# A state space model computed by parts of four tokens instead of token by token

## The chip, the cores and the metric

The kernel runs on one core of a Trainium2 chip. The metric is the device time of one execution in microseconds (us); of several runs the median counts. The core has TensorE (PE, matrix products), VectorE (DVE), ScalarE (ACT), GpSimd (POOL) and SyncE (SP, which issues most DMAs). Each engine works through its own list of instructions strictly in order.

## What is computed

256 tokens of width 1024 go through two blocks of two layers each. The change concerns the second block. Each of its layers is a feed-forward, a token mixer and another feed-forward, with norms and a modulation between. The token mixer contains a state space model on 512 of its channels, in 32 groups of 16 channels with 64 complex states each:

```python
def token_mixer(h, w_in, ...):
    u, q, k, v, f, g_a, g_b = jnp.split(h @ w_in, cuts, axis=-1)
    y_ssm = s5_ssm(u, a_re, a_im, log_dt, b_re, b_im, c_re, c_im, d_skip)
    z_val, z_gate = jnp.split(jax.nn.gelu(y_ssm) @ glu_w, 2, axis=-1)
    y_a = z_val * jax.nn.sigmoid(z_gate)
    y_b = forgetting_attention(q, k, v, f + forget_b) @ attn_w_out
    return (jax.nn.sigmoid(g_a) * y_a + jax.nn.sigmoid(g_b) * y_b) @ w_out

def s5_ssm(u, ...):
    lam_bar = jnp.exp(lam * dt)                     # per group and state, complex
    bu = einsum('blgn,gpn->blgp', u, b_bar)         # 16 inputs -> 64 states, each token
    # states[t] = lam_bar * states[t-1] + bu[t], t over the 256 tokens
    y = real(einsum('gnp,blgp->blgn', c, states))   # 64 states -> 16 outputs
    return y + d_skip * u
```

## The kernel before

**Weights.** Everything stays on the core but the weights, which stream from memory as 576 blocks of 128 rows by 1024. `prepare` (L210) issues a block's DMA on SP into `wr` (L223), ScalarE casts it to the high part `wh` (L229), and VectorE computes the low part `wl = wr - wh` (L236). The pools hold four `wr`, five `wh` and four `wl`. `group` (L255 to L266) makes 24 products of 256 columns from a block, three for each pair of tiles (`xh·wh`, `xl·wh`, `xh·wl`), into tiles `g` of PSUM. The modulation (L496) is computed on VectorE beside this, a step of 128x1024 at a time, from `mraw`.

**Feed-forward.** Groups of gate and up products alternate; behind an up group, VectorE multiplies its results into `act` (L440), ScalarE casts them to `ah` (L367), VectorE computes `al` (L368), and the down products follow.

**Token mixer** (`mixer2`, L1241). First the projection of `u`, then `settle` (L131 to L138), which finishes the normalised activations: for each of eight tiles a step into a buffer `xs` of a ring of two, ScalarE's rounding to `xh`, and a step to `xl`. L1279 scales `u` by the norm `rho` (L404), L1280 adds a bias, and `split` makes a high and a low part of it. A narrow product (`narrow`, L306 and L311) in four column groups gives the forget gates. The projections of v, q, k and two gates follow, with the state space model and the attention between them.

**State space model.** `ssm_params` (L1075) prepares each layer's coefficients: a table of rotations (cosine `c` and sine `z`) for 128 tokens, and the scaled matrix `cT`. Layer 0's is emitted in the block's first feed-forward, layer 1's at the start of its layer, with five DMAs of 512 KB on POOL. `ssm_pair` (L1128) works 16 times a layer, on two groups of 64 states: four DMAs for each two pairs gather `u` into `ux` (L1145); two products (L1147) give the inputs of 128 states at 256 tokens, real and imaginary; VectorE turns them with the table (L1133), runs the recurrence as scans of 128 tokens (L1158) in two halves with a small turning step between (L1166, L1168), and turns the states back (L1133); two float32 products in a group of 32 columns (L1179, L1180) give the outputs. When four pairs are through, `ydone` (L1293) takes over.

**Order.** A planner in the kernel (class `Order`, L1549) gives every instruction a price, schedules the program as a list with these prices, several times forward and backward, and fixes the shortest plan's order on each engine. Tiles of one ring are handed out in the order in which the code was written.

Of the kernel before, what the change touches and what calls it, by code (L numbers as in the profile page):

```python
# [8 lines left out]
F32 = mybir.dt.float32  # L9
F32R = mybir.dt.float32r  # L10
# [4 lines left out]
P = 128  # L15
# [18 lines left out]
DN_WIDTH = 512  # L34

# [106 lines left out]
class Kern:  # L142
    def __init__(s, nc, tc, ctx, d):
        s.nc, s.tc, s.d = nc, tc, d
        s.blocks, s.made, s.used, s.ready = all_blocks(), 0, 0, []
        s.off = 0
        s.n = 0
        s.make = s.rest = s.later = None
        s.credit = s.share = s.hshare = 0.0
        s.todo = [(l, j) for l in range(DEPTH) for j in range(72)]  # L150
        s.px = s.sc_ = None
        pool = lambda name, bufs, **kw: ctx.enter_context(tc.tile_pool(name=name, bufs=bufs, **kw))
# [372 lines left out]
    def layer2(s, l, z, sq, last=False, subs=(0, 1, 2)):  # L525
        for i in subs:
            s.mod_done(l, i)
# [490 lines left out]
    def ssm_coef(s, pool, after):  # L1018

        nc, tc = s.nc, s.tc  # L1020
        V, A = nc.vector, nc.scalar
        n = 16 * DEPTH
        s.sr_ = s.const.tile([P, n], F32, name="ssm_r")
        s.spw = s.const.tile([P, 2, 8, n], F32, name="ssm_pw")
        s.scr = s.const.tile([P, n], F32, name="ssm_cr")
        s.sci = s.const.tile([P, n], F32, name="ssm_ci")
        r, pw, cr, ci = s.sr_, s.spw, s.scr, s.sci
# [9 lines left out]
        A.activation(out=r, in_=a, func=AF.Exp)  # L1037
        sh = t1("sh")
        sn, cn = pw[:, 1, 0, :], pw[:, 0, 0, :]
# [5 lines left out]
        V.tensor_scalar(out=r1, in0=r, scalar1=1.0, scalar2=None, op0=ALU.add)  # L1045
# [5 lines left out]
        tt(xi, r, sn, ALU.mult)  # L1051
# [13 lines left out]
        for e in range(1, 8):  # L1065
            c0, s0, c1, s1 = pw[:, 0, e - 1, :], pw[:, 1, e - 1, :], pw[:, 0, e, :], pw[:, 1, e, :]
# [5 lines left out]
    def first_params(s, pool, after):  # L1072
        s.ssmp = s.ssm_params(0, after)

    def ssm_params(s, l, after=None):  # L1075
# [3 lines left out]
        V, G, PE = nc.vector, nc.gpsimd, nc.tensor  # L1079
        js = slice(16 * l, 16 * l + 16)  # L1080
        bT = s.t(s.lp, [P, 16, 2, P], "sbT", F32R)
        cT = s.t(s.lp, [P, 2, 16, 32], "scT")
        tb = s.t(s.lp, [P, 2, 16, P], "stb")
        w = s.t(s.lp, [P, 4, P], "stw")
        cr, ci = s.scr[:, js], s.sci[:, js]
        tt = lambda e, o, a, b, op: e.tensor_tensor(out=o, in0=a, in1=b, op=op)

        flat, rows = tb.rearrange("p i j t -> p (i j t)"), bT.rearrange("p j i m -> p (j i m)")
        if after is not None:
            V.tensor_copy(out=flat[:, 0:1], in_=after)  # L1090
        for n in range(4):
            o, part = n % 2 * BLK, slice(n * BLK, (n + 1) * BLK)
            b = flat[:, o:o + BLK]
            G.dma_start(out=b, in_=s.d["ssmb"][l, :, part])
            nc.scalar.copy(out=rows[:, part], in_=b)
            tt(V, rows[64:, part], b[64:], rows[64:, part], ALU.subtract)

        part = lambda o: flat[:, 2 * BLK + o:2 * BLK + o + 512].rearrange("p (j n) -> p j n", j=16)
        c0, c1, v = part(0), part(512), part(1024)
        G.dma_start(out=flat[:, 2 * BLK:3 * BLK], in_=s.d["ssmc"][l])  # L1100
        bc = lambda v: v.unsqueeze(2).to_broadcast([P, 16, 32])
        tt(V, cT[:, 0], c0, bc(cr), ALU.mult)
        tt(V, v, c1, bc(ci), ALU.mult)
        tt(V, cT[:, 0], cT[:, 0], v, ALU.subtract)
        tt(V, c0, c0, bc(ci), ALU.mult)
        tt(V, c1, c1, bc(cr), ALU.mult)
        V.scalar_tensor_tensor(out=cT[:, 1], in0=c0, scalar=-1.0, in1=c1, op0=ALU.mult, op1=ALU.subtract)
        c, z = tb[:, 0], tb[:, 1]
        G.memset(c[:, :, 0:1], 1.0)
        G.memset(z[:, :, 0:1], 0.0)  # L1110
        for e in range(7):
            m = 1 << e
            n = min(16, 4 * P // m)
            for j in range(0, 16, n):
                jj = slice(j, j + n)
                pc = s.spw[:, 0, e, js][:, jj].unsqueeze(2).to_broadcast([P, n, m])
                ps = s.spw[:, 1, e, js][:, jj].unsqueeze(2).to_broadcast([P, n, m])
                c0, z0, c1, z1 = c[:, jj, 0:m], z[:, jj, 0:m], c[:, jj, m:2 * m], z[:, jj, m:2 * m]
                v = w.rearrange("p j t -> p (j t)")[:, :n * m].rearrange("p (j t) -> p j t", j=n)
                tt(V, c1, c0, pc, ALU.mult)  # L1120
                tt(V, v, z0, ps, ALU.mult)
                tt(V, c1, c1, v, ALU.subtract)
                tt(V, z1, c0, ps, ALU.mult)
                tt(V, v, z0, pc, ALU.mult)
                tt(V, z1, z1, v, ALU.add)
        return bT, cT, tb

    def ssm_pair(s, l, pool, u, n, done):  # L1128

        nc = s.nc  # L1130
        V, G, PE = nc.vector, nc.gpsimd, nc.tensor
        bT, cT, tb = s.ssmp
        tt = lambda e, o, a, b, op: e.tensor_tensor(out=o, in0=a, in1=b, op=op)  # L1133
        q, jm, odd = n // 8 * 2 + n % 2, n % 8 // 2, n % 2
        j = 4 * q + jm
        jj = 16 * l + j
        c, z = tb[:, 0, j, :], tb[:, 1, j, :]
        xp = s.mps()
        rows = slice(32 * jm, 32 * jm + 32)

        if not odd:
            s.ux = s.t(pool, [P, 2, T], "ux", F32, 2)
            for i in range(2):
                for r in range(2):
                    nc.sync.dma_start(out=s.ux[64 * r + 32 * i:64 * r + 32 * i + 32], in_=u[i][rows, q:q + 2, :])  # L1145
        for i in range(2):
            PE.matmul(xp[:, i * T:(i + 1) * T], bT[:, j, i, :], s.ux.bitcast(F32R)[:, odd], start=True, stop=True)  # L1147
        halves = lambda v: v.rearrange("p (i a t) -> p i a t", i=2, a=2)
        both = lambda v: v.unsqueeze(1).unsqueeze(1).to_broadcast([P, 2, 2, P])
        a, b, st = [s.t(pool, [P, 2 * T], n, bufs=2) for n in ("pa", "pb", "st")]  # L1150
        xp, a4, b4, st = halves(xp), halves(a), halves(b), halves(st)
        a, b = [v.rearrange("p (i t) -> p i t", i=2) for v in (a, b)]
        tt(V, a4, xp, both(c), ALU.mult)
        tt(V, b4, xp, both(z), ALU.mult)
        tt(V, a[:, 0], a[:, 0], b[:, 1], ALU.add)
        tt(V, a[:, 1], a[:, 1], b[:, 0], ALU.subtract)
        rb = s.sr_[:, jj:jj + 1].to_broadcast([P, P])
        scan = lambda i, h, v: V.tensor_tensor_scan(out=st[:, i, h], data0=rb, data1=a4[:, i, h], initial=v,  # L1158
                                                    op0=ALU.mult, op1=ALU.add)
        for i in range(2):  # L1160
            scan(i, 0, 0.0)

        cw, zw = [s.spw[:, i, 7, jj:jj + 1] for i in range(2)]
        turned, first = [s.t(pool, [P, 2], n, bufs=2) for n in ("tw", "fw")]
        last = st[:, :, 0, P - 1]
        V.tensor_scalar(out=turned, in0=last, scalar1=zw, scalar2=None, op0=ALU.mult)  # L1166
        for i, op in ((0, ALU.subtract), (1, ALU.add)):
            V.scalar_tensor_tensor(out=first[:, i:i + 1], in0=last[:, i:i + 1], scalar=cw, in1=turned[:, 1 - i:2 - i],  # L1168
                                   op0=ALU.mult, op1=op)
        for i in range(2):  # L1170
            scan(i, 1, first[:, i:i + 1])
        tt(V, a4, st, both(c), ALU.mult)
        tt(V, b4, st, both(z), ALU.mult)
        tt(V, a[:, 0], a[:, 0], b[:, 1], ALU.subtract)
        tt(V, a[:, 1], a[:, 1], b[:, 0], ALU.add)
        if jm == 0 and not odd:
            s.yp = s.px.tile([P, 512], F32, tag="px", name=s.nm("yp"))
        o = s.yp[rows, odd * T:(odd + 1) * T]
        PE.matmul(o, cT[:, 0, j, :], a[:, 0], start=True, stop=False, tile_position=(0, 32 * jm))  # L1179
        PE.matmul(o, cT[:, 1, j, :], a[:, 1], start=False, stop=True, tile_position=(0, 32 * jm))  # L1180
        if jm == 3:
            done(q, s.yp[:, odd * T:(odd + 1) * T])
# [58 lines left out]
    def mixer2(s, l, h, done):  # L1241
# [4 lines left out]
        with tc.tile_pool(name=s.nm("m2"), bufs=1, reuse_waits="tile") as pool:  # L1246
# [26 lines left out]
            uh = gb.bitcast(F32R)[:, 4:]  # L1273
# [19 lines left out]
            def ydone(f, ps):  # L1293
# [10 lines left out]
                half(gh[:, f, :], gl[:, f, :], y)  # L1304
# [33 lines left out]
            pair = lambda j: s.ssm_pair(l, pool, (gb[:, 4:], gl32), j, ydone)  # L1338
# [529 lines left out]
```

## Time and profile before

| | before |
|---|---|
| median of 3 runs | 1986.65 us (1985.58 to 1990.12) |
| profiled execution | 1980.18 us |
| its span | 1978.4 us |
| TensorE busy | 1883.6 us, 95% |
| VectorE busy | 1619.5 us, 82% |
| ScalarE busy | 1052.3 us, 53% |
| granted TensorE clock, mean | 0.975 |

The page divides the span by engines, and names the chain of work that ended last. Windows of it tell for a stretch how long each engine was busy; groups of instructions give the mean price of one; the timeline gives starts, from which one reads what a row really costs, since matrix products overlap at their ends.

### The profile page before, as it was taken

What the parts mean: (1) busy time and instruction counts of PE and PEld (TensorE: products, weight loads), DVE (VectorE), ACT (ScalarE), POOL (GpSimd) and SP (SyncE); (2) the same over time, 40 slices, a digit from 0 to 9 for tenths busy, and PEclk for the clock granted to TensorE, in tenths of its full rate; (3) what the DMA queues carried; (4) which work ended last, traced back from release to release, by engine and by line L of the source; (5) the groups of instructions that cost most, each with busy time, mean ns of one, the idle gap of its engine ahead of it and who ended that gap; (6) DMA issues with size and microseconds to landing.
All of it is one profiled execution on the core that took longest, in us unless ns stands there. A gap on an engine that the chain in (4) does not pass through costs nothing.

```text
span 1978.4 us, 37727 instructions
## 1 busy us (share of the span) xinstructions
PE 1883.6 (95%) x14826; PEld 1794.6 (91%) x14826; DVE 1619.5 (82%) x3120; ACT 1052.3 (53%) x1933; POOL 8.5 (0%) x24
## 2 busy tenths in 40 slices
PE   7999999899999999998988999999999998999998
PEld 6999999899899989998766999998999876799997
DVE  7988886998977787988988999979775998887554
ACT  6665544675554465446343665546454633465443
POOL 0000000000000000000000000000000000000000
PEclk8999999999999999999988999999999998999999
DMA  5434887543587868774333658774877423354553
GB/s 187 144 108 153 284 281 273 181 135 113 213 281 270 287 217 307 269 256 144 126 102 105 228 182 309 254 264 160 288 265 245 134 97 106 105 190 154 184 187 116
DMA packets 110242, 390.97 MB, mean 198 GB/s; under 512 B 12912, under 2 KB 13424, under 8 KB 110064
## 3 DMA queue, kind: packets, MB, share of 16 engines
q1 hardware_dynamic: 108336, 382.93, 57.1%
q0 software_dynamic: 1440, 5.24, 0.8%
q8 instruction: 116, 1.90, 0.4%
q14 instruction: 62, 0.51, 0.1%
q10 hardware_dynamic: 288, 0.39, 0.1%
HBM read 383.27 MB, written 1.05 MB: 194 GB/s over the span
## 4 chain that ended last, share of the span: by engine, by line
PE 79%; DVE 12%; ACT 4%; DMA 2%; issue 1%; SPq 0%; DVEq 0%; ACTq 0%
PE g L266 69%; PE g L286 3%; DVE wl L236 3%; DVE pa L1133 2%; DVE st L1158 1%; DMA mraw<-in_modw 1%; DVE pb L1133 1%; ACT wh L229 1%; DMA wr<-in_wstream 1%; DVE xs L131 1%; PE yp L1180 1%; PE m L845 1%; PE m L840 1%; PE m L1235 0%; PE yp L1179 0%
## 5 line engine op out<-in xcount | busy, mean ns | idle before, releaser
L266 PE MATMUL g<-xh,wh 128*128 128x256 f32 (+1 forms) x3264 | 921.3, 287 | 31.1 <-ACT xh L137 9.0
L266 PE MATMUL g<-xl,wh 128*128 128x256 f32 x3264 | 920.8, 285 | 0.1
L266 PE MATMUL g<-xh,wl 128*128 128x256 f32 (+1 forms) x3264 | 909.9, 285 | 1.0 <-DVE wl L236 0.8
L236 DVE TENSOR_TENSOR wl<-wr,wh 128x1024 fp32r<-128x1024 f32 (+1 forms) x576 | 694.5, 1213 | 181.4 <-PE g L266 89.4
L229 ACT CAST wh<-wr 128x1024 fp32r<-128x1024 f32 (+1 forms) x528 | 551.9, 1047 | 547.0 <-PE g L266 233.1
L266 PEld LDWEIGHTS g<-xh,wh 128*128 128x128 f32 x3264 | 617.8, 191 | 43.6 <-ACT xh L137 9.7
L266 PEld LDWEIGHTS g<-xl,wh 128*128 128x128 f32 x3264 | 623.1, 191 | 4.6 <-issue 3.9
L266 PEld LDWEIGHTS g<-xh,wl 128*128 128x128 f32 x3264 | 617.0, 192 | 5.1 <-DVE wl L236 2.8
L266 PE MATMUL g<-ah,wl 128*128 128x256 f32 x880 | 245.6, 280 | 0.0
L266 PE MATMUL g<-al,wh 128*128 128x256 f32 x880 | 245.1, 279 | 0.0
L266 PE MATMUL g<-ah,wh 128*128 128x256 f32 x880 | 244.6, 279 | 0.0
L496 DVE SCALAR_TENSOR_TENSOR mraw<-mraw,siluc 128x1024 f32<-128x1024 f32 x144 | 175.8, 1221 | 42.5 <-DMA mraw<-in_modw 42.0
L266 PEld LDWEIGHTS g<-al,wh 128*128 128x128 f32 x880 | 165.4, 188 | 0.0
L266 PEld LDWEIGHTS g<-ah,wl 128*128 128x128 f32 x880 | 165.0, 188 | 0.0
L266 PEld LDWEIGHTS g<-ah,wh 128*128 128x128 f32 x880 | 164.4, 187 | 0.0
L367 ACT CAST ah<-act 128x256 fp32r<-128x256 f32 x132 | 49.9, 405 | 51.5 <-DVE act L440 51.0
L440 DVE TENSOR_TENSOR act<-g,sg 128x256 f32<-128x256 f32 x132 | 51.8, 418 | 13.2 <-PE g L266 11.4
L427 ACT ACTIVATE sg<-g 128x256 f32<-128x256 f32 x108 | 40.0, 385 | 36.2 <-PE g L266 35.9
L368 DVE TENSOR_TENSOR al<-act,ah 128x256 fp32r<-128x256 f32 x132 | 52.0, 419 | 5.5 <-ACT ah L367 3.9
L1133 DVE TENSOR_TENSOR pa<-pa,pb 128x256 f32<-128x256 f32 x128 | 48.7, 418 | 0.8
L266 PE MATMUL g<-gl,wh 128*128 128x256 f32 x128 | 35.7, 281 | 0.0
L266 PE MATMUL g<-v,wl 128*128 128x256 f32 x128 | 35.6, 281 | 0.0
(439 smaller groups left out, 2147.8 us busy)
## 6 DMA issues: line engine op xcount, KB each, us to landing
wr<-in_wstream SPq DMA_DIRECT2D x568, 512.0 KB, 4.6
mraw<-in_modw SPq DMA_DIRECT2D x144, 512.0 KB, 4.2
stb<-in_ssmb POOLq DMA_DIRECT2D x8, 512.0 KB, 5.8
wr<-in_wstream SPq DMA_DIRECT2D x8, 256.0 KB, 4.6
ux<-gb SPq DMA_DIRECT2D x32, 64.0 KB, 4.0
ux<-gl SPq DMA_DIRECT2D x32, 64.0 KB, 3.3
stb<-in_ssmc POOLq DMA_DIRECT2D x2, 512.0 KB, 8.4
x<-in_x SPq DMA_DIRECT2D x2, 256.0 KB, 4.8
```

Source lines behind the costliest of these rows:

```text
L131: nc.vector.scalar_tensor_tensor(out=a, in0=s.z[:, k, :], scalar=s.gains[:, k:k + 1], in1=s.rho, op0=ALU.mult, op1=ALU.mult)
L229: nc.scalar.copy(out=hi[:, :n], in_=raw[:, :n])
L236: e.tensor_tensor(out=lo[:, :n], in0=raw[:, :n], in1=hi[:, :n], op=ALU.subtract)
L266: nc.tensor.matmul(ps[c][:, :x.shape[-1]], wt, x, start=(bi == 0 and k == 0 and i == 0), stop=(bi == len(specs) - 1 and k == n - 1 and i = ...
L286: nc.tensor.matmul(ps[h], x(k0 + k)[:, h * P:(h + 1) * P], wt[:, k, :], start=(k0 == 0 and k == 0 and i == 0), stop=(k0 + k == kt - 1 and ...
L367: s.nc.scalar.copy(out=out_h, in_=src)
L368: s.nc.vector.tensor_tensor(out=out_l, in0=src, in1=out_h, op=ALU.subtract)
L427: nc.scalar.activation(out=a, in_=gp[c][:, :T], func=AF.Silu)
L440: nc.vector.tensor_tensor(out=a, in0=up[c][:, :T], in1=sg[c], op=ALU.mult)
L496: nc.vector.scalar_tensor_tensor(out=w, in0=w, scalar=1.0, in1=s.sc_, op0=ALU.mult, op1=ALU.mult, accum_out=s.mod[l][:, j:j + 1])
L840: PE.matmul(yp[:, i * P:(i + 1) * P], Rm[:, i, :], ut[:, 1, i, :], start=True, stop=True)
L1133: tt = lambda e, o, a, b, op: e.tensor_tensor(out=o, in0=a, in1=b, op=op)
```

## The change

The recurrence runs over 64 parts of four tokens each. Per part, with `lam` for the state's factor and four inputs u0 to u3, the state at the end is lam^4 times the one before, plus lam^3·b·u0 + lam^2·b·u1 + lam·b·u2 + b·u3. So the inputs of a part become one product (a row for each token and channel, 64 rows of tokens by 32 channels), a scan has 64 steps, and the outputs of a part's four tokens are products with the state at the end of the part before (`cp`) and with the part's own inputs (`tz`, a triangle of 4 by 4 blocks).

- `ssm_pair` (16 a layer) is replaced by `ssm_tile` (4 a layer), each for eight groups of 16 channels: eight float32 products of 128x64 (`mi`), the same turning steps on 512 columns, eight scans of 64, and 16 + 32 float32 products of 32 rows by 64 columns, in four column groups.
- `u` is stored by part, through a buffer of the ring `xs`; it is no longer split. 16 DMAs a layer gather it into `up` (32 a layer gathered `ux`).
- `ssm_params` makes `mi`, `cp` and `tz`: 48 steps of 128x512 on VectorE, 32 transposes and 128 products of 32 rows on TensorE, 26 copies on ScalarE. It is emitted in the block's feed-forwards: layer 0's in the first, layer 1's in the second of layer 0. It loads two blocks of 512 KB, on SP.
- `ssm_coef`, in the setup, computes powers of `lam` up to the fourth, with three more exponentials.

```diff
@@ layer2
         for i in subs:
+            if i != 1 and (l if i == 0 else l + 1) == s.next_ssm < DEPTH:
+                s.later = lambda pool, after, n=s.next_ssm: s.ssm_params(n, pool, after)
+                s.next_ssm += 1
...
@@ ssm_params
+        nc.sync.dma_start(out=c, in_=s.d["ssmc"][l])
+        nc.sync.dma_start(out=b, in_=s.d["ssmb"][l].rearrange("p (i j r) -> p i j r", i=2, j=16))
...
+        for e in range(SL):
+            lr, li = lam[0][e], lam[1][e]
+            tt(re[e + 1], re[0], lr, ALU.mult)
+            tt(v, im[0], li, ALU.mult)
+            tt(re[e + 1], re[e + 1], v, ALU.add)
+            tt(im[e + 1], im[0], lr, ALU.mult)
+            tt(v, re[0], li, ALU.mult)
+            tt(im[e + 1], im[e + 1], v, ALU.subtract)
...
+        for j in range(0, 16, 2):
+            tp = s.mps()
+            for n in range(4):
+                PE.transpose(tp[:, n * P:(n + 1) * P], a[:, j + n // 2, n % 2].rearrange("p t r -> p (t r)"), s.ident)
+            A.copy(out=mi[:, j:j + 2], in_=tp.rearrange("p (j i m) -> p j i m", j=2, i=2))
...
+        for j in range(0, 16, 4):
+            ps = s.mps()
+            for jj in range(4):
+                for i in range(2):
+                    for t in range(SL):
+                        PE.matmul(ps[32 * t:32 * t + 32, jj * P + 32 * t:(jj + 1) * P], b[:, i, j + jj],
+                                  cp[:, i, j + jj, 0:SL - t].rearrange("p e r -> p (e r)"), start=i == 0, stop=i == 1,
+                                  tile_position=(0, 32 * t))
...
@@ ssm_pair / ssm_tile
-        for i in range(2):
-            PE.matmul(xp[:, i * T:(i + 1) * T], bT[:, j, i, :], s.ux.bitcast(F32R)[:, odd], start=True, stop=True)
+        for jm in range(4):
+            for i in range(2):
+                o = i * T + jm * NP
+                PE.matmul(xp[:, o:o + NP], mi[:, 4 * q + jm, i], u[:, 4 * q + jm], start=True, stop=True)
...
+        for jm in range(4):
+            jj = 16 * l + 4 * q + jm
+            for i in range(2):
+                part = slice(jm * NP, (jm + 1) * NP)
+                V.tensor_tensor_scan(out=st[:, i, part], data0=s.sr4[:, jj:jj + 1].to_broadcast([P, NP]),
+                                     data1=a[:, i, part], initial=0.0, op0=ALU.mult, op1=ALU.add)
...
-        PE.matmul(o, cT[:, 0, j, :], a[:, 0], start=True, stop=False, tile_position=(0, 32 * jm))
-        PE.matmul(o, cT[:, 1, j, :], a[:, 1], start=False, stop=True, tile_position=(0, 32 * jm))
+        for t in range(SL):
+            for jm in range(4):
+                rows = slice(32 * jm, 32 * jm + 32)
+                PE.matmul(y[rows, t * NP:(t + 1) * NP], tz[:, 4 * q + jm, t], u[:, 4 * q + jm], start=t == 0, stop=False,
+                          tile_position=(0, 32 * jm))
+        for i in range(2):
+            for t in range(SL):
+                for jm in range(4):
+                    rows = slice(32 * jm, 32 * jm + 32)
+                    PE.matmul(y[rows, t * NP + 1:(t + 1) * NP], cp[:, i, 4 * q + jm, t + 1],
+                              a[:, i, jm * NP:(jm + 1) * NP - 1], start=False, stop=i == 1 and t == SL - 1,
+                              tile_position=(0, 32 * jm))
...
@@ mixer2
-                V.tensor_tensor(out=u[:, c, :], in0=gp[c][:, :T], in1=rho, op=ALU.mult)
-                A.activation(out=u[:, c, :], in_=u[:, c, :], func=AF.Identity, bias=cc)
-                s.split(uh[:, c, :], gl[:, c, :], u[:, c, :])
+                a = s.t(s.misc, [P, T], "xs")
+                V.tensor_tensor(out=a, in0=gp[c][:, :T], in1=rho, op=ALU.mult)
+                A.activation(out=u[:, c, :].rearrange("p (t m) -> p t m", t=SL), in_=by_part(a), func=AF.Identity,
+                             bias=cc)
+            for t in range(SL):
+                for jm in range(4):
+                    nc.sync.dma_start(out=up.rearrange("p (c j) m -> p c j m", j=4)[32 * t:32 * t + 32, :, jm],
+                                      in_=u[32 * jm:32 * jm + 32, :, t * NP:(t + 1) * NP])
...
-            pair(0)
+            part = lambda q: s.ssm_tile(l, pool, up, q, ydone)
             proj([1536 + c * P for c in range(4)], plain(lambda c: v[:, c, :]))
-            pair(1)
-            pair(2)
             Vt = s.values(pool, v)
+            part(0)
             for i, t in enumerate((q, k)):
                 proj([512 * (i + 1) + c * P for c in range(4)], plain(grow(t)))
-                for j in range(3 + 2 * i, 5 + 2 * i):
-                    pair(j)
+                part(1 + i)
```

In VectorE's list of before, the coefficients of layer 0 stand in the first feed-forward of block 2, mixed with its weights (L236 is a weight block's low part, L1086 a step of the coefficients, L496 one of the modulation):

```order
L1086 TENSOR_TENSOR scT_9554<-stb_9555,ssm_cr 128x512
L496 SCALAR_TENSOR_TENSOR mraw_10337,mod_2606<-mraw_10337,siluc 128x1024
L236 TENSOR_TENSOR wl_10333<-wr_10331,wh_10332 128x1024
L1086 TENSOR_TENSOR stb_9555<-stb_9555,ssm_ci 128x512
L1086 TENSOR_TENSOR scT_9554<-scT_9554,stb_9555 128x512
L236 TENSOR_TENSOR wl_10366<-wr_10364,wh_10365 128x1024
```

Between two weight steps there stand one or two steps of the coefficients. After, the same place on VectorE (L241 is the low part, L1116 a step of the coefficients), from the third weight block of the run on:

```order
L241 TENSOR_TENSOR wl_9934<-wr_9932,wh_9933 128x1024
L1116 TENSOR_TENSOR smi_9570<-scp_9571,ssm_lam 128x512
L1116 TENSOR_TENSOR scp_9571<-scp_9571,ssm_lam 128x16x32
L1116 TENSOR_TENSOR scp_9571<-scp_9571,smi_9570 128x16x32
L241 TENSOR_TENSOR wl_9964<-wr_9962,wh_9963 128x1024
L1116 TENSOR_TENSOR smi_9570<-scp_9571,ssm_lam 128x512
L1116 TENSOR_TENSOR scp_9571<-scp_9571,ssm_lam 128x16x32
L1116 TENSOR_TENSOR scp_9571<-scp_9571,smi_9570 128x16x32
```

Behind the last weight step 25 rows L1116 follow one another; in the second feed-forward, for layer 1, the pattern is the same.

On TensorE after, at the same place, these rows follow the last product of that fourth weight block (L1159 is a transpose of the coefficients, `stb` is what the last rows L1116 wrote):

```order
L271 MATMUL g_10006<-xl_9143,wh_9963 128x256
L271 MATMUL g_10006<-xh_9142,wl_9964 128x256
L1159 MATMUL m_9628<-cst,stb_9572 128x128 x4
L1159 MATMUL m_9634<-cst,stb_9572 128x128 x4
L1159 MATMUL m_9640<-cst,stb_9572 128x128 x4
L271 MATMUL g_10146<-xh_9142,wh_10008 128x256
L1159 MATMUL m_9646<-cst,stb_9572 128x128 x4
```

TensorE had only weight products here; now transposes stand ahead of the next block's, and 120 of the 128 products of 32 rows follow them.

At the start of a mixer, VectorE's list of before, from the first step behind `rho` on (L131 and L138 are steps of `settle`, L1279 scales `u`):

```order
L131 SCALAR_TENSOR_TENSOR xs_11851<-z_141,modA_2607,rho_11680 128x256
L131 SCALAR_TENSOR_TENSOR xs_11855<-z_141,modA_2607,rho_11680 128x256
L1279 TENSOR_TENSOR u_11721<-g_11727,rho_11680 128x256
L138 SCALAR_TENSOR_TENSOR xl_11637<-xs_11851,mod_2605,xh_11636 128x256
L138 SCALAR_TENSOR_TENSOR xl_11637<-xs_11855,mod_2605,xh_11636 128x256
L131 SCALAR_TENSOR_TENSOR xs_11859<-z_141,modA_2607,rho_11680 128x256
L1279 TENSOR_TENSOR u_11721<-g_11728,rho_11680 128x256
```

After, the end of that stretch on VectorE (L135 and L142 are `settle`, L1339 scales `u`):

```order
L135 SCALAR_TENSOR_TENSOR xs_12118<-z_141,modA_2607,rho_11918 128x256
L278 TENSOR_REDUCE cc_12137<-g_11969 128x1
L142 SCALAR_TENSOR_TENSOR xl_11875<-xs_12114,mod_2605,xh_11874 128x256
L142 SCALAR_TENSOR_TENSOR xl_11875<-xs_12118,mod_2605,xh_11874 128x256
L1339 TENSOR_TENSOR xs_12124<-g_11966,rho_11918 128x256
L1339 TENSOR_TENSOR xs_12129<-g_11967,rho_11918 128x256
```

All 16 rows of `settle` stand ahead of the first L1339; before, L1279 was the third row behind `rho`.

## Rows read from the trace of the kernel before

**Rows 1.** The page: busy time and count by engine; shares of the last chain.
```profile
PE 1883.6 (95%) x14826; PEld 1794.6 (91%) x14826; DVE 1619.5 (82%) x3120; ACT 1052.3 (53%) x1933; POOL 8.5 (0%) x24
PE 79%; DVE 12%; ACT 4%; DMA 2%; issue 1%; SPq 0%; DVEq 0%; ACTq 0%
```

**Rows 2.** Windows: length, busy time of each engine, granted clock, DMA share, GB/s.
```profile
731.50:754.30 22.80, 22.80 (x194) 22.80 (x193) 18.20 (x27) 10.57 (x16) 1.19 (x2) 1.00 0.78 273
921.20:924.60 3.40, 3.40 (x39) 2.77 (x40) 3.40 (x10) 2.54 (x8) 0.00 (x0) 0.50 0.01 2
923.10:1138.30 215.20, 197.17 (x1392) 169.38 (x1388) 194.71 (x433) 105.96 (x205) 1.63 (x3) 0.95 0.46 149
1556.00:1772.00 216.00, 199.67 (x1402) 169.28 (x1395) 190.57 (x430) 104.31 (x203) 0.00 (x0) 0.94 0.41 135
```

**Rows 3.** Groups on VectorE, 700 to 1800 (both mixers): busy, mean ns | idle before.
```profile
L1133 DVE TENSOR_TENSOR pa<-pa,pb 128x256 f32<-128x256 f32 x128 | 48.7, 418 | 0.8
L1158 DVE TENSOR_TENSOR_SCAN st<-ssm_r,fw,pa 128x128 f32<-128x128 f32 x64 | 27.4, 469 | 0.0
L1158 DVE TENSOR_TENSOR_SCAN st<-ssm_r,pa 128x128 f32<-128x128 f32 x64 | 23.5, 408 | 0.0
...
L1133 DVE TENSOR_TENSOR pa<-m,stb 128x512 f32<-128x512 f32 x32 | 21.9, 686 | 14.1 <-PE m L1147 14.1
```

**Rows 4.** Groups on TensorE in the first mixer, 919 to 1138.
```profile
L1180 PE MATMUL yp<-pa,scT 128*32 128x256 f32 x32 | 10.5, 412 | 3.3 <-DVE pa L1133 3.3
L1179 PE MATMUL yp<-pa,scT 128*32 128x256 f32 x32 | 10.3, 405 | 8.7 <-DVE pa L1133 8.7
L1147 PE MATMUL m<-ux,sbT 128*128 128x256 f32 x32 | 7.5, 320 | 0.6 <-ACT pT L1231 0.6
```

**Rows 5.** Timeline at the first mixer's start: start, duration, engine, line, out<-in.
```profile
919.04 0.37 ACT L404 COPY rho<-m 128x256 f32<-128x256 f32 x1 [0.84 <-PE m L359]
...
920.58 0.41 DVE L1279 TENSOR_TENSOR u<-g,rho 128x256 f32<-128x256 f32 x1
...
921.14 1.91 PE L306 MATMUL g<-z,sqb 128*32 128x256 f32 x16 [2.14 <-DVE u L1279]
...
922.75 0.47 PE L311 MATMUL g<-mod,sqb 128*32 128x2 f32 x16
...
923.15 0.58 PE L266 MATMUL g<-xh,wh 128*128 128x256 f32 x1
```

**Rows 6.** The same mixer: gathers; the query projection's start to the end, all and L266.
```profile
923.84 1.22 SPq L1145 DMA_DIRECT2D ux<-gb  x2
...
937.41:1137.55 200.14, 183.24 (x1277) 155.63 (x1278) 181.29 (x398) 93.28 (x184) 1.63 (x3) 0.95 0.44 142
...
937.41:1137.55 200.14, 138.70 (x1056) 131.56 (x1056) 0.95 0.44 142
```

**Rows 7.** DMA issues: KB each, median us from issue to landing.
```profile
wr<-in_wstream SPq DMA_DIRECT2D x568, 512.0 KB, 4.6
```

**Rows 8.** Timeline of VectorE in the first feed-forward of block 2.
```profile
731.40 0.75 DVE L440 TENSOR_TENSOR act<-g,sg 128x256 f32<-128x256 f32 x2
...
793.33 1.23 DVE L236 TENSOR_TENSOR wl<-wr,wh 128x1024 fp32r<-128x1024 f32 x1
794.47 0.68 DVE L1086 TENSOR_TENSOR scT<-stb,ssm_cr 128x512 f32<-128x512 f32 x1
795.07 1.22 DVE L496 SCALAR_TENSOR_TENSOR mraw<-mraw,siluc 128x1024 f32<-128x1024 f32 x1
...
798.07 0.69 DVE L1086 TENSOR_TENSOR scT<-scT,stb 128x512 f32<-128x512 f32 x1
798.78 1.23 DVE L236 TENSOR_TENSOR wl<-wr,wh 128x1024 fp32r<-128x1024 f32 x1
```

**Rows 9.** Timeline of TensorE: eight transposes of the attention, and what follows.
```profile
951.31 1.03 PE L1191 MATMUL m<-cst,v 128*128 128x128 f32 x8
952.10 0.36 PE L266 MATMUL g<-xh,wh 128*128 128x256 f32 x1
```

More of the change, by code (lines that the diff above doesn't have):

```diff
@@ L1064, in ssm_coef, with twice @@
         tt(ci, ci, den, ALU.mult)
-        for e in range(1, 8):
-            c0, s0, c1, s1 = pw[:, 0, e - 1, :], pw[:, 1, e - 1, :], pw[:, 0, e, :], pw[:, 1, e, :]
+        def twice(c0, s0, c1, s1):
             tt(w, s0, s0, ALU.mult)
@@ L1070, in ssm_coef @@
             V.scalar_tensor_tensor(out=s1, in0=c0, scalar=2.0, in1=s0, op0=ALU.mult, op1=ALU.mult)
-    def first_params(s, pool, after):
-        s.ssmp = s.ssm_params(0, after)
-    def ssm_params(s, l, after=None):
+        at = lambda e: (cs[:, 0, e], cs[:, 1, e])
+        pt = lambda e: (pw[:, 0, e], pw[:, 1, e])
+        twice(*at(0), *at(1))
+        twice(*at(1), *pt(0))
+        for e in range(1, 6):
+            twice(*pt(e - 1), *pt(e))
+        (c1, s1), (c2, s2), (c3, s3) = at(0), at(1), at(2)
@@ L1088, in ssm_params @@
[L1088 to L1096, printed above, removed]
@@ new lines, in ssm_params @@
+        nc.sync.dma_start(out=c, in_=s.d["ssmc"][l])
+        nc.sync.dma_start(out=b, in_=s.d["ssmb"][l].rearrange("p (i j r) -> p i j r", i=2, j=16))
+        c0, c1 = half(c[:, 0:512]), half(c[:, 512:1024])
+        re, im = [[cp[:, i, :, e] for e in range(SL + 1)] for i in range(2)]
+        tt(re[0], c0, bc(cr), ALU.mult)
+        tt(v, c1, bc(ci), ALU.mult)
+        tt(re[0], re[0], v, ALU.subtract)
+        tt(c0, c0, bc(ci), ALU.mult)
+        tt(c1, c1, bc(cr), ALU.mult)
+        V.scalar_tensor_tensor(out=im[0], in0=c0, scalar=-1.0, in1=c1, op0=ALU.mult, op1=ALU.subtract)
@@ new lines, in ssm_params @@
+        for i in range(2):
+            A.copy(out=a[:, :, i, SL - 1], in_=b[:, i])
+        for e in range(SL - 1):
+            lr, li = lam[0][e], lam[1][e]
+            ar, ai = a[:, :, 0, SL - 2 - e], a[:, :, 1, SL - 2 - e]
+            tt(ar, b[:, 0], lr, ALU.mult)
+            tt(v, b[:, 1], li, ALU.mult)
+            tt(ar, ar, v, ALU.subtract)
+            tt(ai, b[:, 1], lr, ALU.mult)
+            tt(v, b[:, 0], li, ALU.mult)
+            tt(ai, ai, v, ALU.add)
+        for j in range(0, 16, 2):
[3 more added lines that the diff above has]
+            A.copy(out=mi[:, j:j + 2], in_=tp.rearrange("p (j i m) -> p j i m", j=2, i=2))
@@ new lines, in ssm_params @@
+        tz = tb[:, 0:2048].rearrange("p (j t r) -> p j t r", j=16, t=SL)
+        for t in range(1, SL):
+            G.memset(tz[32 * t:32 * t + 32, :, 0:t], 0.0)
+        for j in range(0, 16, 4):
[6 more added lines that the diff above has]
+                                  tile_position=(0, 32 * t))
+            p4 = ps.rearrange("p (j t r) -> p j t r", j=4, t=SL)
+            for t in range(SL):
+                rows = slice(32 * t, 32 * t + 32)
+                A.copy(out=tz[rows, j:j + 4, t:], in_=p4[rows, :, t:])
@@ L1126, in ssm_params @@
-        return bT, cT, tb
-    def ssm_pair(s, l, pool, u, n, done):
-        nc = s.nc
[L1131 to L1137, printed above, removed]
+            pc, ps = [s.spw[:, i, e, js].unsqueeze(2).to_broadcast([P, 16, m]) for i in range(2)]
@@ L1167, in ssm_pair @@
[L1167 to L1177, printed above, removed]
```

155 lines of the change are left out of this document (78 added, 77 removed).

## The prediction

> **What bounds the kernel now.** I read the page first. TensorE is busy for 95% of the span, and the chain that ended last is 79% TensorE and 12% VectorE [rows 1]: nearly all time is products of weight blocks, and VectorE owns the rest. Then the windows [rows 2]. In a stretch of feed-forward (731.50 to 754.30) TensorE is busy for 22.80 of 22.80 us and VectorE for 18.20: TensorE bounds it, and VectorE has a fifth to spare. In the two mixers (923.10 and 1556.00) TensorE is busy for 197.17 of 215.20 and 199.67 of 216.00 us, while VectorE is busy for 194.71 and 190.57: there VectorE is close to full, and TensorE waits some 16 to 18 us. That is where the change takes work away. The prices of that work are in the groups of VectorE [rows 3] and TensorE [rows 4].
>
> **What goes in a mixer.** Each number is for one layer of two. VectorE: 64 sums of 418 ns (26.8 us), 64 products of some 686 ns (43.9), 32 + 32 scans of 469 and 408 ns (28.1) [rows 3], with smaller turning steps some 103 us busy. The new tile does the same eight products and sums on a tile of 512 columns, four times instead of 16: 4 × (4 × 0.686 + 4 × 0.418) = 17.7 us, and 32 scans of 64 columns that I put at 0.3 us each (an estimate below the 408 ns for 128 columns), 9.6: 27 us. VectorE then has some 119 us of work in a mixer of about 200, and is no longer its bound. TensorE: the products L1179, L1180 and L1147 are 10.3 + 10.5 + 7.5 us busy, with 8.7 + 3.3 + 0.6 us of idle time in front [rows 4]; by starts, where overlapping tails count once, they take 24 us, and 12.6 us of waits.
>
> **What comes in its place on TensorE.** One record of L1179 is 256 columns of float32 from start to start in about 0.27 us (its busy mean is 405 ns with the overlapping tail [rows 4]), two records per product. For 64 columns that is 0.068 us a record, 0.135 a product. A tile has 8 products over all columns (1.1 us) and 48 in four column groups, which is 1.6 us if four run abreast and 6.5 if not. That four run abreast rests on L306: 16 records of 256 columns, in four column groups, took 1.91 us [rows 5] while the granted clock was 0.50, the lower of its two levels [rows 2]; one after another at that clock they would take about 16 × 0.54 = 8.6. So 2.7 us a tile, and I take 3.4 for the switches between the two kinds, 13.6 for four tiles; serial it is 7.6 a tile. For tiny products the nearest row is L311: 16 records of 2 columns in 0.47 us at half clock [rows 5], so 0.06 us a product of two records even there, and 48 of them 2.8 us.
>
> The Trainium skill speaks against such products: "TensorEngine Tiling (Array Packing)", section "Instruction Overhead", says that each matmul has about 60 cycles of overhead, and that no factor should be taken from a dimension that is small already. If these came on top for all 112 records of a tile (0.025 us each at 2.4 GHz, an estimate from that page), the eight tiles would cost 22 us more, and the sum below would be 2033. Row L311, at 0.06 us for two records at half clock, contains whatever such overhead there is and stays well under that when four run side by side, so by the row it does not.
>
> **The start of a mixer.** The state space inputs now pass through a buffer of the two-deep ring that the normalised activations use too, so the order puts all 16 settling steps ahead of L1339, where before they alternate with L1279. Before: rho begins at 919.04 (ready 919.4), the first L1279 at 920.58, the narrow product L306 at 921.14 right behind the release of its buffer, the value projection at 923.15 [rows 5]. The settling steps are 16 steps of 256 columns, at the 418 ns of a sum [rows 3] or a little more, say 0.45, 7.2 us with no gap, less the two that already stand ahead (0.9) and the evacuations: the narrow product starts about 7.2 us behind rho instead of 1.7, so +5.5. With the tile at the front the query projection, which began at 937.41 [rows 6], 18.0 us behind rho, begins at about 24.3 plus a tile. Sixteen gathers stand on SP's queue ahead of the query's weights. Two issues take 1.22 us [rows 6], so they last 9.8; the inputs are complete some 9 us behind rho, the weights are then issued at 19, land 4.6 later [rows 7], and need a cast and a difference (2.2): 26, hidden behind value projection and tile 0 (27.7). If that cover goes, the cost is the difference, up to 5 us.
>
> **The sum for a mixer.** Before, 937.41 to 1137.55, 200.14 us: TensorE is busy for 183.24, so 16.9 are waits, and 138.70 of the busy time are the 1056 block products [rows 6]. Counted by starts, with the overlapping tails once, these are 134.7 (at the warm pitch of 22.80/192 = 0.118 us they would be 124.6; the rest is half clock after waits and switches of kind), and what is left, 48.5, is 24.1 for state space and 24.3 for attention. After: 129.6, 23, 13.6 and 6 of waits, so 172.2: −27.9. With the later start (+5.5, and 0.5 for what lies between) it is −22 a layer. Bounds: −10 (the waits stay) and −36 (no wait is left and TensorE stays at full clock).
>
> **What is added in the feed-forward.** The preparation of the coefficients moves ahead of both mixers: for layer 0 into the first feed-forward, at 731, for layer 1 into the second. VectorE's order there is no longer one coefficient step between two weight steps: it has 53 rows in one run, with 48 steps of 512 columns and only four weight differences and one step of the modulation in it, and 25 steps of the 48 come last, uninterrupted. TensorE's next row behind the fourth block is the transposes, which need the last of these steps. That is the step on which my forecast rests. Prices: two such steps start 0.60 us apart when independent (794.47 to 795.07) and 0.71 when the second needs the first (798.07 to 798.78) [rows 8]; mixed as here, I take 0.64. The activations that come ahead of the run end at about 737.2 (from 731.40, when the first sum behind the group before starts [rows 8]: four sums and two differences at 0.38 and three weight steps at 1.14, as 793.33 to 794.47). So the run ends at 737.5 + 48 × 0.64 + 4 × 1.14 + 1.2 = 774. TensorE has eight weight blocks until then, 192 products that take 22.80 us, to 754.3 [rows 2]: it idles 19.7 us in that stretch, wherever the four weight steps split it. Now 0.6 us are lost there; +19. Bounds +14 (a run at 0.60 that starts two steps early) and +23 (at 0.71). That VectorE saves as much work elsewhere in the feed-forward gives nothing back, since TensorE bounds it.
>
> Then TensorE itself: 32 transposes at 0.10 us (eight of L1191 went from 951.31 to 952.10 [rows 9]), 3.2 us; they share three buffers with ScalarE's copies. 128 products of 32 rows and 128 to 32 columns, mean 80: 0.27 × 2 × 80/256 = 0.17 us each, 5.4 in all if four run abreast and evenly, 8.6 if each four takes the time of its longest: 7.5. Half clock and buffers: 2.3. So +13, bounds 9 and 28 (one after another). ScalarE's copies of these results come partly ahead of the casts that the mixer's start waits for: six of them, at about the 0.37 us of the copy at 919.04 [rows 5]: +2, bounds 0 and 4. POOL's DMAs, which go, and the setup's powers and exponentials lie beside other work (the last chain gives ScalarE 4% [rows 1]): 0.
>
> **How the numbers follow.** Per layer 19 + 13 + 2 − 22 = +12, for two +24. The profiled execution is 1980.18, so its like would be 2004; the median of the runs shown is 6.5 above it, 1986.65 + 24 = 2011.
>
> **Rivals.** *Faster:* the mixer's fall is larger than what the feed-forward loses. Place: the mixer from the query projection to its end. If all waits go and the array stays warm (124.6 + 21 + 11 + 1), it is −42 + 6 = −36, and with the run at its short end (+14 + 9 + 0) a layer nets −13: 1961; at the middle of both about 1975. It decides at a gain of 34 a layer. For it: VectorE is nearly full there now. Against it: 16 to 18 us of waits in all are there to be won. Chance 0.14. *Serial:* the column groups don't overlap: +14 per layer in the preparation and +17 in the mixer, 2073. Against it L306. Chance 0.06. *The mixer stays:* VectorE's relief doesn't show since others of the waits end last (ScalarE's exponentials, the gathers), gain −10: 2035. Chance 0.11. *Covered:* the long run is hidden, since VectorE reaches it early, and nets against the mixer, 1983 to 1990: chance 0.07. The forecast has 0.62, with a range of its own of 1995 to 2030 from the bounds above.
>
> The range is 1982 to 2045: it leaves out most of the faster rival and the serial one. A measurement can tell about 0.2% (4 us) from no change. Faster 0.14; same 0.07; slower 0.79.
>
> **What would show it.** TensorE idle for about 20 us at 754 and again in the second feed-forward, released by VectorE's L1116; L1159 behind that; products of 64 columns in groups of four starts; VectorE at some 60% in the mixers, these some 22 us shorter; narrow products 7 us behind rho. Wrong if no gap above 10 us stands in front of L1159, or if a mixer is more than 34 us shorter.

## The result

The changed kernel is slower: 1996.85 us against 1986.65 us in the medians of five runs each, a ratio of 1.0054 (95% interval 1.0036 to 1.0073). Run again, the changed kernel had 1996.3 us and a ratio of 1.0062 (1.0047 to 1.0078). The forecast was 2011, 24 us more than before; it was 10 to 11 us. The sign and the range held, and so did the mechanism of the loss. The size did not, mainly because the waits that the forecast left in the mixers are gone.

The page of the changed kernel, busy time and shares of the last chain (as in [rows 1]):

```profile
PE 1888.2 (94%) x16106; PEld 1830.1 (92%) x16106; DVE 1516.6 (76%) x2826; ACT 1075.8 (54%) x1976; POOL 8.4 (0%) x20
PE 84%; DVE 8%; ACT 3%; DMA 3%; issue 2%; SPq 0%; DVEq 0%; ACTq 0%
```

VectorE has lost 103 us of work in the whole, and its share of the chain fell from 12% to 8%; TensorE's share rose from 79% to 84%. The time went up all the same. TensorE's waits, summed over the changed kernel (what it waited for: us in all, times, longest):

```profile
PE m L1159 <- DVE stb L1116: 28.5, 4, 12.7
PE g L311 <- DVE sqb L303: 13.4, 1, 13.4
...
PE g L311 <- DVE xs L1339: 6.1, 2, 3.0
```

The largest wait is new: the transposes of the coefficients (L1159) wait for the vector steps (L1116), in both feed-forwards. L311 behind L1339 is the narrow product at each mixer's start, where the kernel before waited for L1279; that wait grew from 4.2 us in all to 6.1. None of the waits of [rows 4], L1179 and L1180 for VectorE, has a successor: no wait for a state space step is left in the mixers.

I took a second trace of each kernel. Where the time is, by stages, for the first and the second trace, in us; a stage goes from the end of rho's copy to the first product of the next norm's sums (L578, L586 after):

| stage | before | after | difference | forecast |
|---|---|---|---|---|
| first feed-forward of block 2 | 184.3, 182.8 | 210.6, 211.0 | +26.3, +28.1 | +32 |
| second feed-forward | 180.2, 180.3 | 216.7, 215.1 | +36.5, +34.8 | +32 |
| from a feed-forward to the mixer's rho, both | 37.5, 37.4 | 34.8, 35.2 | −2.7, −2.2 | +4 |
| first mixer | 218.1, 218.5 | 191.8, 192.9 | −26.4, −25.6 | −22 |
| second mixer | 218.1, 222.9 | 191.8, 190.4 | −26.3, −32.6 | −22 |
| all the rest | 1140.1, 1144.7 | 1152.6, 1150.3 | +12.5, +5.5 | 0 |
| span | 1978.4, 1986.7 | 1998.3, 1994.8 | +19.9, +8.1 | +24 |

The first trace of before (1980.18 us) lies 5 to 6.5 us below its medians, the changed kernel's first (2000.42) 3.6 above; the second pair, +8.1 us, stands nearer to the +10 to +11 of the medians. Nearly all of the difference in the row "all the rest" has come by the end of rho's copy ahead of the first feed-forward of block 2: 716.4 and 720.7 us before, 727.6 and 726.0 after.

Two stretches carry the account. In the first feed-forward, VectorE's run begins at 745.55 and ends behind 781.47 (timeline of VectorE, the changed kernel):

```profile
745.55 0.69 DVE L1116 TENSOR_TENSOR scp<-stb,ssm_cr 128x512 f32<-128x512 f32 x1
746.14 0.69 DVE L1116 TENSOR_TENSOR smi<-stb,ssm_ci 128x512 f32<-128x512 f32 x1
...
781.47 0.69 DVE L1116 TENSOR_TENSOR stb<-stb,smi 128x512 f32<-128x512 f32 x1
782.08 0.42 DVE L373 TENSOR_TENSOR al<-act,ah 128x256 fp32r<-128x256 f32 x1
```

On TensorE, at the same place:

```profile
780.16 0.48 PE L1159 MATMUL m<-cst,stb 128*128 128x128 f32 x1 [12.68 <-DVE stb L1116]
782.21 2.61 PE L1159 MATMUL m<-cst,stb 128*128 128x128 f32 x11 [1.58 <-DVE stb L1116]
784.83 1.91 PE L1159 MATMUL m<-cst,stb 128*128 128x128 f32 x8
...
789.25 5.21 PE L1170 MATMUL m<-scp,sbb 128*32 128x128 f32 x184
```

12.68 + 1.58 us of idle time stand in front of the transposes. And the windows of the changed kernel (length, busy time of each engine, granted clock, DMA share, GB/s), of that wait, of the first mixer from rho on, and of the mixer from the query projection on:

```profile
759.40:782.21 22.81, 8.53 (x65) 7.93 (x65) 22.29 (x34) 2.11 (x2) 0.00 (x0) 0.75 0.10 39
...
955.80:1147.60 191.80, 188.28 (x1814) 175.72 (x1813) 133.02 (x268) 108.15 (x206) 0.00 (x0) 0.98 0.45 152
...
988.20:1147.57 159.37, 158.90 (x1551) 148.54 (x1550) 111.93 (x214) 90.66 (x176) 0.00 (x0) 1.00 0.48 166
```

The last row answers [rows 6]: TensorE is busy for 158.90 of 159.37 us, at a granted clock of 1.00. Before, the same part had 16.9 us of waits in 200.14, at 0.95.

### The profile page after: what moved, and what is told of

It is laid out like the page before. It is cut to its first block, busy times and chain, and to the rows that moved or that the text cites. A ratio compares the mean times of both kernels' runs of the same rounds, so it can differ in the third digit from the quotient of the medians.

```text
span 1998.3 us, 40034 instructions
## 1 busy us (share of the span) xinstructions
PE 1888.2 (94%) x16106; PEld 1830.1 (92%) x16106; DVE 1516.6 (76%) x2826; ACT 1075.8 (54%) x1976; POOL 8.4 (0%) x20
## 4 chain that ended last, share of the span: by engine, by line
PE 84%; DVE 8%; ACT 3%; DMA 3%; issue 2%; SPq 0%; DVEq 0%; ACTq 0%
PE g L271 72%; PE g L291 3%; DVE wl L241 2%; DMA mraw<-in_modw 1%; DMA wr<-in_wstream 1%; DVE smi L1116 1%; DVE stb L1116 1%; PE m L1205 1%; DVE scp L1116 1%; ACT wh L234 1%; PE m L853 1%; PE m L848 1%; DVE xs L135 1%; PE m L1159 0%; PE m L1293 0%
## 5 line engine op out<-in xcount | busy, mean ns | idle before, releaser
L241 DVE TENSOR_TENSOR wl<-wr,wh 128x1024 fp32r<-128x1024 f32 (+1 forms) x576 | 697.0, 1214 | 253.4 <-PE g L271 134.4
L271 PEld LDWEIGHTS g<-xl,wh 128*128 128x128 f32 x3264 | 626.1, 192 | 10.2 <-DVE xl L390 8.9
L373 DVE TENSOR_TENSOR al<-act,ah 128x256 fp32r<-128x256 f32 x132 | 52.3, 420 | 12.0 <-ACT ah L372 10.2
L1159 PE MATMUL m<-cst,stb 128*128 128x128 f32 x64 | 12.9, 364 | 28.5 <-DVE stb L1116 28.5
L1159 PEld LDWEIGHTS m<-cst,stb 128*128 128x128 f32 x64 | 10.8, 192 | 29.5 <-DVE stb L1116 29.5
```

The costliest lines, as they stand in the source:

```text
L241: e.tensor_tensor(out=lo[:, :n], in0=raw[:, :n], in1=hi[:, :n], op=ALU.subtract)
L271: nc.tensor.matmul(ps[c][:, :x.shape[-1]], wt, x, start=(bi == 0 and k == 0 and i == 0), stop=(bi == len(specs) - 1 and k == n - 1 and i = ...
L373: s.nc.vector.tensor_tensor(out=out_l, in0=src, in1=out_h, op=ALU.subtract)
L1159: PE.transpose(tp[:, n * P:(n + 1) * P], a[:, j + n // 2, n % 2].rearrange("p t r -> p (t r)"), s.ident)
```

## The experiments

**Both kernels a second time.** No edit.

> The changed kernel as it is, a second time, for a second trace. In the first pair of traces the changed kernel is 19.9 us longer, of which 10.2 us have come by the 217th weight block, ahead of all that the change touches by its code, and 3.9 more between the first mixer and the second preparation. Theory (the planner's new order of the first block costs this, so it belongs to the program): the 217th block again starts at least 8 us later than in the trace of before, and the span is 1993 to 2000. Rival (the two executions differed by chance): it starts less than 4 us later.

> The kernel before as it is, a second time, for a second trace. The changed kernel's second trace has the first block again 8.7 us longer than the one trace of before, at the 217th weight block. Theory (that is the order of the new program): in this second trace of before, that block starts within 2 us of 744.2. Rival (the one trace of before, 1980.18 us where the medians are 1985 to 1987, was a lucky execution): it starts 4 us later or more, and that much of the loss in the first block is not the change's.

The changed kernel: 1996.3 us, span 1994.8; its 217th weight block began at 753.0. The kernel before: 1988.46 us (one run), span 1986.7; the block began at 749.6, not 744.2. So, as far as one more trace tells, 5.3 of the 8.7 us in the first block were the first trace of before, and 3.4 are the new program's: the theory in the first expectation overstated them, and the rival in the second holds. In the second trace of before the second mixer lasted 222.9 us instead of 218.1, with nearly the same waits (L1179 4.9 and 5.0 us). What differs is TensorE's clock; the window of that mixer in the first trace and in the second:

```profile
1552.60:1770.70 218.10, 200.27 (x1410) 169.53 (x1411) 192.67 (x437) 105.38 (x206) 0.00 (x0) 0.94 0.41 133
```

```profile
1557.50:1780.40 222.90, 205.91 (x1411) 173.06 (x1412) 192.55 (x437) 105.17 (x205) 0.00 (x0) 0.92 0.40 130
```

**No preparation.** The preparation's 48 steps, transposes and products are left out, so the state space part isn't computed; its instructions in the mixers run, on zeros:

```diff
-        (DMAs of ssmc and ssmb, 48 steps, 32 transposes, 128 products, their copies)
+        G.memset(mi, 0.0)
+        G.memset(cp, 0.0)
+        G.memset(tb[:, 0:2048], 0.0)
```

> Leaves out the preparation: the matrices mi, cp and tz are zeroed on GpSimd, only the table is computed, so the state space part is not computed. Theory (the preparation costs 28 and 31 us in the two feed-forwards): 55 to 62 us below the changed kernel, 1935 to 1942, which is what the mixers alone give. Rival (the feed-forwards' loss is in part a shift that the mixers would have had anyway, as weights come late): less than 45 us.

Measured 1927.4 us, 69 below the changed kernel, ratio to before 0.9715 (0.9695 to 0.9734). The feed-forwards fall to 182.5 and 180.3 us, those of before, and the mixers stay at 190.8 and 190.5. So the change's two halves are separate: without the preparation the change gives 57 us, nearly all of it in the mixers, and the preparation takes 69 back. The theory's range ended 7 us short of that, and the rival is excluded.

**The transposes late.** The preparation is cut in two; the second half is written behind the fifth group of the feed-forward and bound to an activation of it:

```diff
+                if s.later2 and g0 == LATE:
+                    s.later2(pool, ah[:, g0, 0:16])
...
-            A.copy(out=a[:, :, i, SL - 1], in_=b[:, i])
+            V.tensor_copy(out=a[:, :, i, SL - 1, 0], in_=after)
+            A.copy(out=a[:, :, i, SL - 1], in_=b[:, i])
```

> The coefficients' transposes, products and table are written behind the fifth group of the feed-forward, and the transposes need an activation of that group; the 48 vector steps stay where they are written. In VectorE's order these steps then stand one to four at a time between weight steps. Theory (TensorE's wait of 14 us a layer in front of the transposes comes from the uninterrupted run): no wait above 3 us there, 24 to 32 us in all gained on the changed kernel, 1965 to 1973. Rival (the preparation's own work on TensorE and the new coefficients' load on VectorE are what costs, and the wait returns elsewhere): within 8 us of the changed kernel.

Measured 1965.81 us, 30.5 below the changed kernel; ratio to before 0.9912 (0.9896 to 0.9928). TensorE's longest waits in its first feed-forward, 728 to 923:

```profile
PE g L272 <- ACT xh L142: 2.4, 1, 2.4
PE m L1182 <- issue: 0.6, 1, 0.6
```

No wait for the vector steps is left. VectorE does the same 48 steps, TensorE the same transposes and products, and the feed-forwards are 194.6 and 198.2 us instead of 210.6 and 216.7: 16.0 and 18.6 us were the price of the order. The other 12 and 18 us (against 182.8 and 180.3) are the work and what goes with it; in the second feed-forward 4.7 of them are TensorE's wait at the start for ScalarE's `xh` (L142), which was 1.9 us before. The theory holds.

**Another buffer for u.** Undone is the use of the settling steps' ring:

```diff
-                a = s.t(s.misc, [P, T], "xs")
+                a = s.t(pool, [P, 2 * T], "pa", bufs=2)[:, :T]
```

> Undoes one part: the buffer through which u passes comes from the ring pa instead of the ring of the settling steps, so L1339 no longer stands behind all 16 settling steps. Theory (the ring puts the narrow product 10 us behind rho, TensorE waits 3.0 us there and runs at half clock): the narrow product starts within 4 us of rho and the two mixers together are 6 to 10 us shorter than in the changed kernel. Rival (TensorE has u's last products to do there anyway, and the value projection waits for the settled activations): under 2 us in all.

Measured 1990.08 us, 6.2 below the changed kernel. At the first mixer's start, timeline of the changed kernel, and then of this one:

```profile
955.42 0.37 ACT L409 COPY rho<-m 128x256 f32<-128x256 f32 x1 [2.09 <-PE m L364]
...
965.91 1.93 PE L311 MATMUL g<-z,sqb 128*32 128x256 f32 x16 [3.05 <-DVE xs L1339]
```

```profile
955.45 0.37 ACT L409 COPY rho<-m 128x256 f32<-128x256 f32 x1 [0.81 <-PE m L364]
...
959.98 1.51 PE L311 MATMUL g<-z,sqb 128*32 128x256 f32 x12 [3.49 <-DVE sqb L303]
```

The narrow product starts 4.2 us behind rho instead of 10.1, a little over the theory's 4, and the mixers last 186.9 and 186.8 instead of 191.8: 9.9 us, at the upper end of the theory. The median has 6.2 of them; 1.7 us were given back between the second feed-forward and the rho of the third (20.4 us, where both traces of the changed kernel have 18.7), where nothing was edited, and where the others went isn't shown.

**Both mends.** The two edits together.

> Both mends together: the transposes written late and bound to an activation of the fifth group, and u's buffer from the ring pa. Theory (the two losses lie in different stretches and add up): 1965.8 less about 6, 1956 to 1962. Rival (the ring's 6 us in the second experiment came from the new order elsewhere): 1964 to 1970.

Measured 1949.73 us, 16 below the late transposes alone; ratio to before 0.9817 (0.9804 to 0.9831). The mixers last 186.2 and 185.0 us (192.6 and 192.3 with the late transposes alone), so 13.7 of the 16 us are there. The rival is excluded, and the theory's 6 us was too small: it took the second experiment's sum, from which something had been given back elsewhere. This version is faster than both kernels, by 1.8% than before and by some 2.3% than the changed one.

**Vector work given back to the mixers.** In each tile one product on VectorE is repeated; its result is the same:

```diff
-        tt(b, two(xp), zq, ALU.mult)
+        for _ in range(29):
+            tt(b, two(xp), zq, ALU.mult)
```

> The changed kernel with one product on VectorE of each tile repeated 28 times more (same result), 4 x 28 steps of 512 columns, about 70 us a mixer, so VectorE's load there is that of before again while TensorE's work is that of after. Theory (the mixers got shorter by 28.5 us since VectorE no longer holds TensorE back, and TensorE's own saving is 24.1 - 14.7 = 9): each mixer is 10 to 18 us longer than in the changed kernel, 2016 to 2032. Rival (fewer, larger steps on TensorE alone give the gain): each mixer under 4 us longer, below 2006.

> As the eighth experiment with 14 repetitions instead of 28: some 35 us of work on VectorE more in each mixer than in the changed kernel. With 28 the mixers became 47 and 48 us longer. Theory A (VectorE's total is the bound: it stays some 40 us below the mixer's length here): under 8 us a mixer, 1996 to 2012. Theory B (each uninterrupted run counts, since weight steps and results behind it wait, as in the feed-forward): 18 to 28 us a mixer, 2032 to 2052.

With 28 repetitions 2096.8 us, mixers of 239.8 and 240.1 us; with 14, 2030.19 us, mixers of 207.2 and 207.8. First mixers, 14 and then 28 repetitions, as windows:

```profile
957.10:1164.30 207.20, 194.54 (x1814) 180.03 (x1813) 165.62 (x324) 108.41 (x206) 0.00 (x0) 0.96 0.43 141
```

```profile
957.60:1197.50 239.90, 202.01 (x1814) 185.69 (x1813) 201.55 (x380) 107.71 (x207) 0.00 (x0) 0.90 0.38 121
```

VectorE's load alone, with TensorE's work untouched, makes a mixer longer than it was before the change (218.1 us with 197.64 us of VectorE); it is the load of before in amount, but not in its places. The eighth experiment's rival is excluded; its theory has the sign, but measured 48 us where it said 10 to 18. TensorE's waits with 28 repetitions, in the first mixer:

```profile
PE m L1268 <- DVE pb L1200: 12.0, 1, 12.0
PE yp L1231 <- DVE y L1360: 9.6, 1, 9.6
PE g L271 <- DVE wl L241: 8.6, 4, 4.7
```

The repetitions stand in a row, and weight differences (L241) and scores (L1268) wait behind them, as in the feed-forward. The first 33 us of added work cost 15.4 us a mixer, at a time when VectorE was busy for 165.62 of 207.20, and the next 36 cost 32.6. So neither theory of the tenth experiment holds: 15.4 us lie between them, and single runs cost something while VectorE's total is still far below the mixer's length. With 28 repetitions the total is still 38 us below it (201.55 of 239.90), though each added microsecond cost nearly one, so it isn't seen to be the bound there either. By the windows, 9.1 of the first 15.4 us are idle time of TensorE and 6.3 are longer busy time of the same 1814 records, at a granted clock of 0.96 instead of 0.98; of the next 32.6 it is 25.2 and 7.5, at 0.90.

**Another order of the same instructions.** The planner mixes forward and backward times with a weight; nothing else is edited, in the kernel before and in the changed one:

```diff
-MIXP = 0.1
+MIXP = 0.15
```

> The kernel before, with one number of the planner changed, the weight by which it mixes forward and backward times (0.1 to 0.15); every instruction is the same and only orders differ. It measures what a new order alone is worth. Theory (the order of the first block moves by chance with any edit): the time differs from before by 3 to 12 us, with the differences at the norms and in the first block's delta rule. Rival (orders of equal plans are worth the same, and the 9 us in the first block come from the edit): within 2 us.

> The changed kernel with the planner's mixing weight at 0.15 instead of 0.1, as in the sixth experiment for the kernel before, where the new order alone cost 11.6 us (0.59%). Theory (an edit also draws a new order, worth some 10 us either way, and that is as large as the change's whole effect): between 1985 and 2010, and more than 3 us away from the changed kernel. Rival (the changed kernel's order is as good as others, only before's was a good one by chance): within 3 us of 1996.5.

The kernel before: 1997.65 us, 11.6 above itself, ratio 1.0059 (1.0041 to 1.0078). The changed kernel: 1997.08, the same as with 0.1. In before's other order the mixers last 225.1 and 227.9 us, 7 and 5 to 10 more than in before's two traces, and not the norms and the first block that the theory named: the first feed-forward's rho ends at 722.6, where before has 716.4 and 720.7. The first mixer as a window, before and then in the other order:

```profile
919.40:1137.50 218.10, 198.33 (x1412) 170.05 (x1413) 197.64 (x440) 107.80 (x211) 1.63 (x3) 0.95 0.45 146
```

```profile
921.70:1146.80 225.10, 205.59 (x1417) 173.32 (x1418) 197.87 (x451) 109.25 (x212) 2.75 (x6) 0.92 0.46 149
```

TensorE is idle for as long as before (19.5 us and 19.8); it is busy for 7.3 us more, at a granted clock of 0.92 instead of 0.95. My theory, that any edit draws an order worth some 10 us either way, holds for before and fell for the changed kernel. At 0.15 the two kernels are equal (ratios 1.0059 and 1.0053 to the same kernel before): the loss of 0.5% is a loss against a good order of before.

## Why the prediction was right in kind and wrong in size

- **The run of vector steps in the feed-forward**: right. 53 rows from 737.5 to 774, 36.5 us, were forecast; they took 745.55 to 782.08, 36.5 us. The steps' pitch was 0.60 and 0.72, as in [rows 8].
- **TensorE's idle time for it**: 19.7 us forecast, 14.3 us measured in front of the transposes. The 192 products ahead of the transposes began 2.5 us ahead of the run of vector steps (743.1), where the forecast had 6.0 (731.5), so they ended nearer to its end; 0.9 us of waits stand among them. In the stage table the two feed-forwards give +63 in both pairs, where the forecast had 64.
- **TensorE's own work for it**: 13 us forecast; in the late version, without waits for the vector steps, the feed-forwards are 12 and 18 us longer than before, 2.8 us of the 18 for the longer wait at the start.
- **Side by side**: right, as L306 had told. By starts, the 256 records of L1237 took 4.3 us, 17 ns each, where L1179 takes 270 for four times the columns. The three groups in the first mixer (busy, mean ns):

```profile
L1205 PE MATMUL m<-up,smi 128*128 128x64 f32 x64 | 8.5, 274 | 0.0
L1237 PE MATMUL yp<-pa,scp 128*32 128x63 f32 x256 | 4.6, 220 | 0.0
L1230 PE MATMUL yp<-up,stb 128*32 128x64 f32 x128 | 3.5, 223 | 0.0
```

  By starts 7.45 + 4.29 + 3.00 = 14.7 us; 13.6 were forecast. The eight products a tile over all columns (L1205) took 7.45, not the 4.4 of 1.1 a tile; the sum is close because 2.8 us had been put down for switches between the kinds. The overhead that "TensorEngine Tiling (Array Packing)" of the Trainium skill gives for each matmul (section "Instruction Overhead"), 22 us in all if it came on top, does not show here: 17 ns between starts is less than the 25 ns that 60 cycles at 2.4 GHz would take (an estimate from that page), so with four groups side by side it does not add up.
- **The mixer, the step that failed.** The forecast left 6 us of waits in each mixer, since 16.9 us of waits had several causes and only 12.6 stood in front of the pairs' products (12.0 of these behind VectorE). From the query projection to the end (988.20 to 1147.57) 0.5 us of waits is left, at a clock of 1.00. Counted by starts as in the prediction, the terms of that part are:

  | | forecast | measured |
  |---|---|---|
  | block products, 1056 | 129.6 | 129.5 |
  | attention | 23 | 20.8 |
  | state space, behind tile 0 | 10.2 | 8.8 |
  | waits | 6 | 0.5 |
  | sum | 168.8 | 159.6 |

  So the waits were mis-sized, by 5.5 us a mixer, and the attention by 2. The product term came out; that it lies 5 us above 124.6 isn't half clock, since the clock was 1.00. Against this the start was longer: the narrow product 10.1 us behind rho, not 7.2, and the query projection 32.4, not 27.7; 6.0 us of state space products stand ahead of it, where tile 0 was put at 3.4. Net −26 to −33 a mixer instead of −22, 9 to 14 us in both; 4.8 us of the 14 are the longer second mixer in the second trace of before. I had the mixer without waits as a bound, −36, and gave it as the faster rival: that the waits went was right there, but its products (124.6), its state space (11) and its start were too short. Why all the waits went together is not shown one by one. The vector load shows that work on VectorE can bring TensorE's waits back (idle time of 3.5, 12.7 and 37.9 us in the first mixer with 0, 14 and 28 repetitions), most of them at other rows than before. VectorE was busy there for 133.02 of 191.80 us, 69%, where some 60% were forecast (119 us): the forecast took durations off a busy time in which overlapping rows count once (in the first mixer the durations of VectorE's rows sum to 227 us before and 148 after, 79 less; its busy time fell by 65).
- **ScalarE's copies**: +2 a layer forecast; the stretch in which they were to cost, from the feed-forward to rho, became 1 us shorter. That is 6 us in all, the second term that was too large.
- **Everything else at nothing**: +12.5 and +5.5 us in the two pairs of traces, nearly all ahead of the second block. It was no term of the sum. What made it is not shown: the setup's `ssm_coef` is edited ahead of that point, and the order is new. Orders do move it: rho ahead of the first feed-forward ends at 722.6 in before's other order, 2 to 6 us later than in its own, and at 723.3 in the changed kernel's other order, 3 to 4 us earlier.
- **The sum.** The second pair of traces: 62.9 for the feed-forwards (forecast 64), −2.2 for the stretches to rho (+4), −58.2 for the mixers (−44), +5.5 for the rest (0): 8.1 before rounding.

## What to carry to other kernels

Work that a planner may put where it likes is not free because its engine has slack on the whole: ask for the longest uninterrupted run of it, and for the row on the other engine that waits for its end. Here binding the consumer to a later event turned a loss of 0.5% into a gain of 0.9% with no instruction saved. And when orders are recomputed with each edit, measure a neutral edit of the order too: in one of the two kernels it was worth as much as the change.

## What I had not expected of the hardware

- The same program, with nearly the same waits, took 4.8 us longer in one mixer at a mean granted clock of 0.92 than at 0.94, more than half of what the two executions of before differ by.
- A float32 transpose of 128x128 took 0.10 us from start to start, one record, where a product with 32 columns of weights has two.
- Gathers of 32 KB between places on the chip, in runs of 256 bytes, landed 1.9 us after their issue (median of 32), faster than before's 64 KB in runs of 1 KB (3.3 and 4.0).
